# First modulations of a transformer block from stationary weight pages, with the first FFN products between them

## The chip, the cores and the metric

The kernel runs on one core of a Trainium2 chip. The metric is the device time of one execution in microseconds; where several executions are timed, the median is given. The core's engines each work through their own instructions in order: TensorE (PE for its products, PEld for the loads of its stationary operand), VectorE (DVE), ScalarE (ACT), GpSimd (POOL), and SyncE (SP), which here asks for the transfers. Sixteen DMA engines carry out what SP asks for.

## What is computed

The reference is one block of a diffusion backbone: 1024 latent tokens x and 256 context tokens ctx, both 1024 channels wide, in fp32. A modulation is a vector of 1024 numbers made from a conditioning vector; there are nine for the latents (from c) and nine for the context (from c_ctx). The first sublayer needs modulations 0 (shift) and 1 (scale):

```python
mods   = split(silu(c)     @ w_ada + b_ada, 9)      # latent tokens
mods_c = split(silu(c_ctx) @ w_ada + b_ada, 9)      # context tokens
h  = x + grid_pos_emb
h  = ffn_sublayer(h,   mods[0],   mods[1],   mods[2],   g_ffn1, w_ffn1_in, w_ffn1_out)
hc = ffn_sublayer(ctx, mods_c[0], mods_c[1], mods_c[2], g_ffn1, w_ffn1_in, w_ffn1_out)
...

def ffn_sublayer(h, shift, scale, gate, g, w_in, w_out):
    hn = rmsnorm(h, g) * (1 + scale) + shift
    a, b = split(hn @ w_in, 2)
    return h + 0.5 * gate * ((silu(a) * b) @ w_out)
```

Behind it come an mLSTM beside a gated chunk mixer, a second such FFN and a last norm. The change leaves all that as it is.

## The kernel before, in words

All activations lie with channels on the 128 partitions: h[tb][d] is the latents' channel block d of 8 in token half tb, hc[d] the context's (256 tokens). An fp32 product is made of three products of rounded parts: each operand is split into a high part (ACT casts) and a low part (VectorE subtracts, `split`, L145 and L146), and `mm3` (L182) issues high x high, high x low and low x high into one PSUM bank.

The head of the program makes modulations 0 and 1 and normalises the context. The 2 x 1024 columns of w_ada are cut into four quarters `qt` of 256 columns of each modulation and four parts `kp` of two row blocks; `ada_page` asks for 32 pieces of 256 KB with runs of 1 KB. Three quarters go over TensorE with silu(c) and silu(c_ctx) as two stationary columns and a page of 512 columns moving (`ada_rows`, L851); the two rows that come out are copied by ACT (`ada_copy`, L855) and turned into columns by four small products (`ada_flip`, L860). The fourth quarter is summed by VectorE (`side`, L792 and L794), transposed, reduced and spread by a product (L798, L799, L868). `ada_done` and `ada_side` add the bias and make the scale; `mod0` (L932 to L935) then applies scale and shift to two context blocks at a time and splits them into `hnc`. The junk products of `idle` (L923) keep TensorE at work meanwhile.

Then the loop over f (22 blocks of the FFN's width) multiplies the context by the first FFN's input weights: two tiles of 128 x 1024 a block (`wa` for a, `wb` for b), 24 products a tile, into the banks pa and pb, two blocks to a bank. `Weights` brings the tiles: `load` asks for one (`raw`, 512 KB), splits it into one of three `hl` buffers and keeps three ahead; every second pair of tiles has its raw page in the pool of the old modulation pages. The last two context blocks are only modulated while the first products run (`last0`). While the loop runs, the pages of x come in (L1020, one channel block in two halves for each f up to 8), the positions are added to them (`add_pos`, L917) and their squares summed for the latents' norm (L209, L210): these jobs stand in the list `todo` and `mm3` issues one after so many products, by a credit that each product adds to. The norm's row of the latents is then made by p (L215) and rb (L231).

The order on TensorE, VectorE and ACT in the head is the one in which the code is written: a `manual_schedule` from the start of the head to the end of f = 0. GpSimd and SP are not under it: the scheduler sets their order there, and that of all engines after it. The page of the positions (`pos`) is asked for (L1006) in the code just behind the head, ahead of the loop.

Of the kernel before, what the change touches and what calls it, by code (L numbers as in the profile page):

```python
# [55 lines left out]
def _build(ctx, tc, nc, a, out):  # L56
# [50 lines left out]
    class Weights:  # L107


        def __init__(self, order, name):  # L110
            self.c = ExitStack()
            self.pool = self.c.enter_context(tc.tile_pool(name=name, bufs=1, reuse_waits="tile"))
            self.order = deque(order)
            self.ready = deque()
            self.held = 0
            self.n = 0

        def load(self):
            n, i, w = self.order.popleft()
            src = a[n][i]  # L120
            if self.n % 4 < 2:
                raw = self.pool.tile([128, w], F32, name="raw", tag="raw", bufs=2)
            else:
                raw = hnp.tile([128, w], F32, name="raw", tag="pg0" if self.n == 2 else "pg1", bufs=8)
# [655 lines left out]
    def ada_load(page, m, hf, k):  # L780
        pgt = page()
        o = m * 1024 + hf * 512
# [53 lines left out]
    NQ = 4  # L836
    QW = 1024 // NQ
    QD = QW // 128
    KP = 512 // QW

    def ada_page(qt, kp, tag):
        pg = hnp.tile([128, KP, 2, QW], F32, name="adapg", tag=tag, bufs=8)
        for i in range(KP):
            src = a["w_ada"][kp * KP + i].rearrange("p (m c) -> p m c", m=9)[:, 0:2, qt * QW:(qt + 1) * QW]
            nc.sync.dma_start(pg[:, i], src)
        return [pg[:, i].rearrange("p m c -> p (m c)") for i in range(KP)]

    def ada_rows(pr, pgs, kp):
        for i, pg in enumerate(pgs):
            k = kp * KP + i  # L850
            T.matmul(pr[0:2, 0:2 * QW], sc2[:, :, k], pg, start=k == 0, stop=k == NKT - 1, skip_group_check=True)  # L851

    def ada_copy(pr):
        row = t2("adrow", shape=(2, 2 * QW))
        S.copy(row, pr[0:2, 0:2 * QW])  # L855
        return row

    def ada_flip(pc, row):
        for j in range(2 * QD):
            T.matmul(pc[:, 2 * j:2 * j + 2], row[:, j * 128:(j + 1) * 128], ident[0:2, 0:2], start=True, stop=True,  # L860
                     skip_group_check=True)

    def ada_side(qt, reds):
        bv = vs_("b_ada").rearrange("p (m d) -> p m d", m=9)
        cs = slice(qt * QD, (qt + 1) * QD)
        p8 = sm_ps("p8")
        for q, red in enumerate(reds):
            T.matmul(p8[:, q * 16:q * 16 + 16], grp4, red[:, 0:16], start=True, stop=True)  # L868
        for q in (1, 0):
            for r in range(4):  # L870
                sl = slice(32 * r, 32 * r + 32)
                V.tensor_add(mods[sl, 0:2, q, cs],
                             p8[sl, q * 16:q * 16 + 16].rearrange("p (m d r) -> p m d r", m=2, r=4)[:, :, :, r], bv[sl, 0:2, cs])
            scale_mod(0, 1, q, "g_ffn1", cs)

    def ada_done(qt, pc):
        sl = slice(qt * QD, (qt + 1) * QD)
        bv = vs_("b_ada").rearrange("p (m d) -> p m d", m=9)
        for q in (1, 0):
            V.tensor_add(mods[:, 0:2, q, sl],  # L880
                         pc[:, 0:4 * QD].rearrange("p (m d q) -> p m d q", m=2, q=2)[:, :, :, q], bv[:, 0:2, sl])
            done = scale_mod(0, 1, q, "g_ffn1", sl)
        return done
# [22 lines left out]
    def load_c(hcp, n):  # L906
        for i, pg in enumerate(hcp):
            nc.sync.dma_start(pg, a["cT"][i * n:(i + 1) * n].rearrange("d p t -> p d t"))
# [20 lines left out]
    def mod0(*ds):  # L929
        ts = [t2("nt")[:, 0:256] for _ in ds]  # L930
        for d, t in zip(ds, ts):
            S.activation(t, hc[d], AF.Identity, bias=mods[:, 0, 1, d:d + 1], scale=smod[:, 0, 1, d:d + 1])  # L932
            S.copy(hnc[d][:, 0, :], t)
        for d, t in zip(ds, ts):
            (V if d % 2 else G).tensor_tensor(hnc[d][:, 1, :], t, hnc[d][:, 0, :].bitcast(F32), ALU.subtract)  # L935

    def scaled0():
        for d in range(NKT):
            V.tensor_tensor(hc[d], hc[d], nct.rb, ALU.mult)
# [3 lines left out]
    sides = [t2("adacc") for _ in range(2)]  # L943

    def side(kp, pgs):
        for i, pg in enumerate(pgs):
            for q in range(2):
                ada_acc(V, sides[q], pg, q, kp * KP + i, kp + i == 0)

    load_c(hcp, 4)  # L950
    pgs = {}
    for qt, kp in ((2, 0), (0, 0), (0, 1), (2, 1), (0, 2), (0, 3), (2, 2), (1, 0), (1, 1), (2, 3), (1, 2), (1, 3),
                   (3, 0), (3, 1), (3, 2), (3, 3)):
        pgs[qt, kp] = ada_page(qt, kp, "pg1" if qt % 2 else "pg0")
    idle(30)
    for d in range(NKT):
        nct.sq(d)
    side(0, pgs[2, 0])
    prs = {0: mm_ps("adr")}
    ada_rows(prs[0], pgs[0, 0], 0)  # L960
    nct.rstd()
    ada_rows(prs[0], pgs[0, 1], 1)
    idle(3)
    side(1, pgs[2, 1])
    ada_rows(prs[0], pgs[0, 2], 2)
    nct.bcast()
    ada_rows(prs[0], pgs[0, 3], 3)
    row = ada_copy(prs[0])
    scaled0()
    side(2, pgs[2, 2])  # L970
    idle(4)
    pc = sm_ps("adc")
    ada_flip(pc, row)
    ada_done(0, pc)
    mod0(0, 1)
    prs[1] = mm_ps("adr")
    for kp in range(NKT // KP):
        ada_rows(prs[1], pgs[1, kp], kp)
    row = ada_copy(prs[1])
    side(3, pgs[2, 3])  # L980
    reds = [cp.tile([128, 32], F32, name="adred", tag="adred", bufs=2) for _ in range(2)]
    for acc, red in zip(sides, reds):
        ada_red(acc, red, 0)
    prs[3] = mm_ps("adr")
    ada_rows(prs[3], pgs[3, 0], 0)
    pc = sm_ps("adc")
    ada_flip(pc, row)
    ada_done(1, pc)
    mod0(2, 3)
    ada_rows(prs[3], pgs[3, 1], 1)  # L990
    ada_side(2, reds)
    for kp in (2, 3):
        ada_rows(prs[3], pgs[3, kp], kp)
    W.load()
    mod0(4, 5)
    row = ada_copy(prs[3])
    W.load()

    def last0():
        pc = sm_ps("adc")  # L1000
        ada_flip(pc, row)
        ada_done(3, pc)
        mod0(6, 7)
        W.load()
# [12 lines left out]
    for f in range(NF):  # L1017
        if 0 < f <= NKT:
            for tb in range(2):
                nc.sync.dma_start(h[tb][f - 1], a["xT"][f - 1, :, tb * 512:(tb + 1) * 512])  # L1020
        if 2 <= f < 2 + NKT:
            for tb in range(2):
# [13 lines left out]
        wa = W.take("w1i", 2 * f)  # L1036
        wb = W.take("w1i", 2 * f + 1)
        if f % 2 == 0:
            pa, pb = mm_ps("pa"), mm_ps("pb")
# [1367 lines left out]
```

## Time and profile before

| | us |
|---|---|
| median of 3 runs | 2641.32 |
| lowest and highest of them | 2641.31, 2643.13 |
| the profiled execution, its own time | 2639.9 |
| its span | 2638.1 |

The groups of the profile give: line, engine and operation, what is written from what (buffer numbers left out), the shape of one instruction, how many; then busy time in us and the mean of one in ns; then idle time of the engine ahead of them and what ended it. A timeline row gives the start, the time and the same names; a row of the chain the start, the time and the place. A row of the windows gives for a stretch of the span the busy time of each engine with its instructions, then the clock granted to TensorE (1.00 is full), the mean busy share of the DMA engines and the GB/s that they moved.

### The profile page before, as it was taken

The numbers are of one execution on the slowest core, as the hardware profiler recorded it, in microseconds if no ns is written. First come the engines' busy times: TensorE is split into PE (matmuls) and PEld (weight loads), VectorE is DVE, ScalarE is ACT, GpSimd is POOL, SyncE is SP. The second block draws the span as 40 slices with busy tenths as digits, with TensorE's granted clock in tenths as the row PEclk, the third lists the DMA queues.
The fourth block names the chain that finished last, engine by engine and source line by source line (L and its number), as shares of the span: only waits on it lengthen the run. The fifth ranks groups of instructions, "written<-read, shape, count | busy, mean of one in ns | idle before, by whom it ended". The sixth has DMA issues, their size and how long they took to land.

```text
span 2638.1 us, 35899 instructions
## 1 busy us (share of the span) xinstructions
PE 2621.8 (99%) x12856; PEld 2205.1 (84%) x12856; DVE 1978.8 (75%) x3546; ACT 1205.6 (46%) x2175; POOL 75.8 (3%) x158
## 2 busy tenths in 40 slices
PE   9999999999999999999999999999999999999998
PEld 6998888888889878888888888888887888888887
DVE  7988688687989646777765878778799766665855
ACT  5664344444347525564443454333346444344433
POOL 0000000000000000000000002221000000000000
PEclk9999999999999999999999999999999999999999
DMA  9833344368587222346653566546341333337644
GB/s 312 311 113 127 128 164 161 117 224 307 169 283 268 77 80 85 111 162 205 196 172 112 166 206 247 180 150 206 125 157 39 128 136 123 113 125 282 199 159 177
DMA packets 200083, 448.54 MB, mean 170 GB/s; under 512 B 20192, under 2 KB 54496, under 8 KB 199904
## 3 DMA queue, kind: packets, MB, share of 16 engines
q1 hardware_dynamic: 199472, 445.85, 49.6%
q8 instruction: 101, 1.65, 0.3%
q14 instruction: 78, 0.64, 0.1%
q10 hardware_dynamic: 432, 0.39, 0.0%
HBM read 324.92 MB, written 121.32 MB: 169 GB/s over the span
## 4 chain that ended last, share of the span: by engine, by line
PE 93%; DVE 2%; issue 2%; DMA 2%; ACT 1%; SPq 0%; POOL 0%; POOLq 0%; ACTq 0%; DVEq 0%
PE qa L412 18%; PE pq L1380 17%; PE po L536 13%; PE qb L412 13%; PE pt L1864 6%; PE pr L1299 6%; PE po L2239 3%; PE pa L182 2%; PE pc L1166 2%; PE pb L182 2%; PE pn L2024 2%; PE pu L1700 1%; PE pn L2022 1%; PE pkc L1359 1%; PE pvc L1456 1%
## 5 line engine op out<-in xcount | busy, mean ns | idle before, releaser
L146 DVE TENSOR_TENSOR ring<-rawq,ring 128x512 fp32r<-128x512 f32 x408 | 281.3, 690 | 221.2 <-ACT ring L145 218.5
L536 PE MATMUL po<-gring,wring 128*128 128x512 f32 (+1 forms) x1896 | 424.0, 384 | 0.1
L536 PEld LDWEIGHTS po<-gring,wring 128*128 128x128 f32 x1896 | 349.4, 188 | 70.8 <-ACT px L693 0.9
L145 ACT CAST ring<-rawq 128x512 fp32r<-128x512 f32 x408 | 253.4, 622 | 309.2 <-PE pq L1380 86.1
L412 PE MATMUL qa<-fc,ring 128*128 128x512 f32 x1056 | 252.3, 389 | 0.0
L412 PEld LDWEIGHTS qa<-fc,ring 128*128 128x128 f32 x1056 | 198.2, 188 | 41.4 <-DVE fc L146 0.4
L1380 PE MATMUL pq<-fc,ring 128*128 128x512 f32 x864 | 207.3, 392 | 0.0
L145 ACT CAST wring<-rw 128x512 fp32r<-128x512 f32 x154 | 95.7, 622 | 216.6 <-PE po L536 184.7
L1380 PEld LDWEIGHTS pq<-fc,ring 128*128 128x128 f32 x864 | 161.4, 188 | 33.0
L1864 PE MATMUL pt<-yp,ring 128*128 128x512 f32 x768 | 184.4, 394 | 0.0
L1864 PEld LDWEIGHTS pt<-yp,ring 128*128 128x128 f32 x768 | 143.0, 188 | 28.2
L146 DVE TENSOR_TENSOR wring<-rw,wring 128x512 fp32r<-128x512 f32 x154 | 105.6, 686 | 80.7 <-ACT wring L145 80.5
L1380 PE MATMUL pq<-fa,ring 128*128 128x512 f32 x576 | 141.9, 394 | 0.0
L1380 PE MATMUL pq<-fb,ring 128*128 128x512 f32 x576 | 136.8, 391 | 0.0
L412 PE MATMUL qa<-fa,ring 128*128 128x512 f32 x528 | 129.6, 395 | 3.5 <-DVE ring L146 3.5
L412 PE MATMUL qa<-fb,ring 128*128 128x512 f32 x528 | 126.8, 390 | 0.0
L412 PE MATMUL qb<-fb,ring 128*128 128x512 f32 x528 | 126.6, 389 | 0.0
L1380 PEld LDWEIGHTS pq<-fb,ring 128*128 128x128 f32 x576 | 107.5, 188 | 22.4 <-issue 0.2
L412 PE MATMUL qb<-fc,ring 128*128 128x512 f32 x528 | 126.2, 389 | 0.0
L412 PE MATMUL qb<-fa,ring 128*128 128x512 f32 x528 | 126.2, 389 | 0.0
L1380 PEld LDWEIGHTS pq<-fa,ring 128*128 128x128 f32 x576 | 106.9, 188 | 21.9 <-DVE ring L146 0.2
L794 DVE SCALAR_TENSOR_TENSOR adacc<-adapg,sc,adacc 128x512 f32<-128x512 f32 x154 | 111.8, 747 | 17.8 <-DMA adapg<-in_w_ada_dram 17.0
(380 smaller groups left out, 4671.5 us busy)
## 6 DMA issues: line engine op xcount, KB each, us to landing
adapg<-in_w_ada_dram SPq DMA_DIRECT2D x144, 256.0 KB, 3.7
fsp<-fhl SPq DMA_DIRECT2D x66, 512.0 KB, 2.7
gring<-fsp SPq DMA_DIRECT2D x66, 512.0 KB, 4.3
raw<-in_w1i_dram SPq DMA_DIRECT2D x44, 512.0 KB, 5.4
graw<-fsp SPq DMA_DIRECT2D x88, 256.0 KB, 3.2
rawq<-in_w1i_dram SPq DMA_DIRECT2D x38, 512.0 KB, 3.7
rawq<-in_w2i_dram SPq DMA_DIRECT2D x38, 512.0 KB, 3.4
fsp<-p SPq DMA_DIRECT2D x66, 256.0 KB, 2.1
```

The lines of the kernel that those rows point to most:

```text
L145: hi = S.copy(hl[:, 0, :], src)
L146: return hi, V.tensor_sub(hl[:, 1, :], src, hl[:, 0, :].bitcast(F32))
L182: T.matmul(pt, x, y, start=first and i == 0, stop=i == n - 1, skip_group_check=True)
L412: T.matmul(pt, hl[:, x, sl], pages[p][k][:, y, :], start=first and i == 0, stop=i == 11, skip_group_check=not first)
L536: T.matmul(pt[:, cs], w[:, x, sl], g[:, y, cs], start=grp and kp == 0 and i == 0, stop=kp == NFP - 1 and i == 2, skip_group_check=not grp)
L794: eng.scalar_tensor_tensor(acc, pgt, sc2[:, q, k:k + 1], acc, ALU.mult, ALU.add)
L1166: T.matmul(pt, hl[d // 4][:, x, sl], g[:, y, :], start=f == 0 and d % 2 == 0 and i == 0, stop=f == NF - 1 and i == 2, skip_group_check=True)
L1299: T.matmul(self.pt[m], pg[:, x, sl], hl[:, y, :], start=first and k == 0 and i == 0, stop=k == 3 and i == 2, skip_group_check=not first)
L1380: T.matmul(pt, hl[:, x, k * 128:(k + 1) * 128], pg[k][:, y, :], start=first and k == 0 and i == 0, stop=k == 3 and i == 2, skip_group_chec ...
L1864: T.matmul(pt, hl[:, x, k * 128:(k + 1) * 128], pg[:, y, :], start=kh + k + i == 0, stop=kh == 1 and k == 3 and i == 2)
L2024: T.matmul(pn[:, 0:257], qi[:, c_, :], self.C[d][:, c_, :], start=False, stop=c_ == 1)
L2239: T.matmul(pt, hl[:, x, k * 128:(k + 1) * 128], FO[p][k][:, y, :], start=first and k == 0 and i == 0, stop=k == 3 and i == 2, skip_group_c ...
```

## The change

Modulations 0 and 1 of the context come from pages of 128 output columns with all 1024 rows. Of the 16 such pages, eleven (`UNITS`, laid out in a tensor w_adaU of their own) are stationary operands: for each of the eight row blocks a product with silu(c) and silu(c_ctx) as two moving columns, so that both modulations come out as columns (`unit`). Five (`SIDE`, w_adaT, transposed) are multiplied with a row and summed by VectorE in one instruction (`side`): the row is silu(c_ctx) spread over the partitions by eight products (`spread`, scB[1]), and later silu(c) (scB[0]), which goes out to memory (scq) and comes back to all partitions. These five sums for silu(c) are jobs in `todo` from f = 2 on, ahead of the additions of positions.

The squares of the context are taken two blocks at a time. Each context block is modulated when its modulations are there, and the products of it with the first four weight tiles follow at once (`first`), between the pages. `Weights` gets a `fetch` that only asks for a tile, five `hl` buffers for three, and keeps five ahead. All transfers of the head, five tiles among them, are written ahead of it in one list. The loop over f begins at 1, and its products at 2. w_ada keeps modulations 2 to 8; ctx is laid out so that its pages are runs of 4 KB.

```diff
-        def load(self):
+        def fetch(self):
             n, i, w = self.order.popleft()
...
-            hl = self.pool.tile([128, 2, w], F32R, name="hl", tag="hl", bufs=3)
+            self.raws.append((n, i, w, raw))
+
+        def load(self):
+            if not self.raws:
+                self.fetch()
+            n, i, w, raw = self.raws.popleft()
+            hl = self.pool.tile([128, 2, w], F32R, name="hl", tag="hl", bufs=5)
             split(hl, raw)
...
-            while self.order and self.held < 3:
+            while (self.raws or self.order) and self.held < 5:
                 self.load()
...
+    for u in ("hc0", (1, 0), "hc1", (1, 1), (0, 0), (1, 2), (0, 1), (1, 3), (0, 2), "W", (0, 3), (1, 4), "W", (0, 4), (1, 5),
+              (0, 5), "W", (1, 6), (0, 6), "W", (1, 7), (0, 7), "W"):
+        if u == "W":
+            W.fetch()
...
+        if u == (1, 2):
+            nc.sync.dma_start(scq, sc2[:, 0, :])
+    nc.sync.dma_start(scB[0], scq.rearrange("p k -> (p k)").partition_broadcast(128))
...
+    def side(m, d, q):
+        V.tensor_tensor_reduce(waste, page[m, d], scB[q], 1.0, vs_("b_ada")[:, m * 8 + d:m * 8 + d + 1], ALU.mult, ALU.add,
+                               mods[:, m, q, d:d + 1])
...
+        for k in range(NKT):
+            T.matmul(col[m, d], page[m, d][:, k * 128:(k + 1) * 128], sc2[:, :, k], start=k == 0, stop=k == NKT - 1,
+                     skip_group_check=True)
...
+    first(0, 1, 3)
+    first(0, 0, 4)
+    first(0, 1, 4)
+    first(1, 0, 0, 1)
+    first(0, 0, 5)
+    unit(1, 7)
+    side(0, 7, 1)
+    unit_done(1, 7)
+    mod0(7)
+    W.load()
...
+    first(0, 0, 7)
+    first(0, 1, 7)
+    W.done(2)
+    first(1, 0, 4, 5, 6, 7)
+    W.done()
+    first(1, 1, 4, 5, 6, 7)
+    W.done()
+    order.close()
 
     nc.sync.dma_start(pos, a["pos"])
...
-    for f in range(NF):
-        if 0 < f <= NKT:
+    for f in range(1, NF):
+        if f <= NKT:
...
         if 2 <= f < 2 + NKT:
+            if f - 2 < len(SIDE):
+                slow(side, *SIDE[f - 2], 0)
             for tb in range(2):
                 slow(add_pos, tb, f - 2)
```

Two places of the order that comes out of this matter below. The first is SP's, from the last modulation page on. Before, the two last pieces of w_ada (adapg) are followed by weight tiles (raw) in the order of use, by the rest of the constants (cst), the positions (pos) and the halves of x (h):

```order
L845 DMA adapg_187<-in_w_ada_dram 128x2x256 x2
L126 DMA raw_386<-in_w1i_dram 128x1024
L126 DMA raw_401<-in_w1i_dram 128x1024
L1007 DMA cst_86<-in_cst_dram 128x384
L126 DMA raw_445<-in_w1i_dram 128x1024
L1006 DMA pos_130<-in_pos_dram 128x320
L126 DMA raw_474<-in_w1i_dram 128x1024
L126 DMA raw_485<-in_w1i_dram 128x1024
L1020 DMA h_112<-in_xT_dram 128x512
L1020 DMA h_120<-in_xT_dram 128x512
```

After, behind the last page (adaT_182) come the broadcast row, the constants, halves of x and then tiles; raw_184 is the first tile of f = 2 (its split is hl_455), while raw_496, raw_513 and raw_611 are its third, its fourth and one of f = 5:

```order
L914 DMA adaT_182<-in_w_adaT_dram 128x1024
L926 DMA scB_136<-scq_139 128x1024
L1063 DMA cst_86<-in_cst_dram 128x384
L1076 DMA h_112<-in_xT_dram 128x512
L1076 DMA h_120<-in_xT_dram 128x512
L1076 DMA h_113<-in_xT_dram 128x512
L1076 DMA h_121<-in_xT_dram 128x512
L127 DMA raw_496<-in_w1i_dram 128x1024
L127 DMA raw_513<-in_w1i_dram 128x1024
L127 DMA raw_611<-in_w1i_dram 128x1024
L1076 DMA h_114<-in_xT_dram 128x512
L127 DMA raw_184<-in_w1i_dram 128x1024
```

Then follow nine more halves of x and five more tiles, the rows below the last of them; here are the positions, and what stands behind (raw_530 and raw_579 are the tiles of f = 4):

```order
L1076 DMA h_125<-in_xT_dram 128x512
L127 DMA raw_902<-in_w1i_dram 128x1024
L1076 DMA h_118<-in_xT_dram 128x512
L1076 DMA h_126<-in_xT_dram 128x512
L1062 DMA pos_130<-in_pos_dram 128x320
L127 DMA raw_935<-in_w1i_dram 128x1024
L1076 DMA h_119<-in_xT_dram 128x512
L1076 DMA h_127<-in_xT_dram 128x512
L378 DMA rawh_1401<-in_w1i_dram 128x1024
L127 DMA raw_530<-in_w1i_dram 128x1024
L127 DMA raw_579<-in_w1i_dram 128x1024
```

The positions moved from the place ahead of all halves of x to one behind 14 of the 16, and the tiles no longer stand in the order of use. 50 transfers now stand ahead of the positions.

The second place is VectorE's, at the end of the head. The semaphores that an instruction waits for stand in brackets; each DMAHW counts every eighth of SP's transfers. Before, the first addition of positions stands behind the last split of the context (hnc_135) and ahead of the splits of the third to fifth tile:

```order
L935 TENSOR_TENSOR hnc_135<-nt_438,hnc_135 128x256 [waits Activation_49]
L917 TENSOR_TENSOR h_112<-h_112,pos_130 128x512 [waits DMAHW3_49,DMAHW0_49]
L146 TENSOR_TENSOR hl_447<-raw_445,hl_447 128x1024 [waits DMAHW7_49,Activation_49]
L146 TENSOR_TENSOR hl_476<-raw_474,hl_476 128x1024 [waits DMAHW1_49,Activation_49]
L146 TENSOR_TENSOR hl_487<-raw_485,hl_487 128x1024 [waits DMAHW2_49,Activation_49]
```

After, it stands behind the last sum of a page for silu(c_ctx), the first for silu(c) and the last split of the context, and ahead of the splits of f = 2 and f = 3:

```order
L937 ISA waste_138,mods_101<-adaT_182,scB_137,vec_84 128x1024 [waits DMAHW0_49,DVE_49]
L937 ISA mods_101 128x1
L955 TENSOR_SCALAR smod_103<-adc_440,bias1_140,vec_84 128x2 [waits PE_49]
L937 ISA waste_138,mods_101<-adaT_147,scB_136,vec_84 128x1024 [waits DMAHW1_49,DVE_49]
L937 ISA mods_101 128x1
L895 TENSOR_TENSOR hnc_135<-nt_451,hnc_135 128x256 [waits Activation_49]
L879 TENSOR_TENSOR h_112<-h_112,pos_130 128x512 [waits DMAHW3_49,DMAHW2_49]
L153 TENSOR_TENSOR hl_455<-raw_184,hl_455 128x1024 [waits DMAHW3_49,Activation_49]
L153 TENSOR_TENSOR hl_493<-raw_491,hl_493 128x1024 [waits DMAHW1_49,Activation_49]
L153 TENSOR_TENSOR hl_498<-raw_496,hl_498 128x1024 [waits DMAHW7_49,Activation_49]
L153 TENSOR_TENSOR hl_515<-raw_513,hl_515 128x1024 [waits DMAHW0_49,Activation_49]
```

The addition kept its place between the context's last split and the next tiles, but its second DMAHW wait is now the count that the transfer of the positions completes (the seventh on DMAHW2).

From the end of the first loop on, the rows of all engines are the same before and after but for the numbers of lines and buffers, and the second request for ctx, whose runs are longer.

More of the change, by code (lines that the diff above doesn't have):

```diff
@@ L966, in _build @@
+    unit(0, 1)
+    unit(1, 3)
     nct.bcast()
[L967 to L993, printed above, removed]
[L994 to L1004 removed]
+    for u in ((1, 0), (1, 1), (0, 1)):
+        unit_done(*u)
```

233 lines of the change are left out of this document (140 added, 93 removed).

## The prediction
> **What bounds the kernel now.** I read the page first, then the chain of work that ended last, then the stage before the chain becomes plain.
>
> ```profile
> span 2638.1 us, 35899 instructions
> PE 2621.8 (99%) x12856; PEld 2205.1 (84%) x12856; DVE 1978.8 (75%) x3546; ACT 1205.6 (46%) x2175; POOL 75.8 (3%) x158
> ...
> 37.38 2.18 PE pa L182 x16
> 39.55 0.98 PE adc L860 x8
> 40.53 2.35 PE pb L182 x18
> ...
> 50.95 2.88 PE pa L182 x24
> 53.83 2.88 PE pb L182 x24
> 56.71 2.88 PE pa L182 x24
> ```
>
> TensorE is busy 99% of the span, and in the chain each weight tile of the context's first FFN (24 products, 2.88 us) follows the last without a gap. I number these tiles n0, n1, ... in the order of use: n0 and n1 are f = 0, and n4 is the first of f = 2. In the chain n4 starts at 50.95; its third product, the first that needs the low half of its weights, comes 2 x 0.12 = 0.24 us later, at 51.2. All that stands on TensorE after n4 is the same before and after the change, as far as the order of instructions tells. So I measure the change by one number: **how much later or earlier does n4's third product run**, plus what TensorE loses behind it.
>
> **The front, which the change rewrites, has cover.** What it adds on TensorE is cheap: the eleven stationary pages are 8 products of 2 columns each, and an fp32 product is two passes, each about one weight load.
>
> ```profile
> 97.47 0.98 PEld L215 LDWEIGHTS p<-ones,acc 128*128 128x128 f32 x8
> L146 DVE TENSOR_TENSOR hl<-raw,hl 128x1024 fp32r<-128x1024 f32 x6 | 7.2, 1224 | 0.7 <-ACT hl L145 0.6
> L794 DVE SCALAR_TENSOR_TENSOR adacc<-adapg,sc,adacc 128x512 f32<-128x512 f32 x14 | 9.6, 746 | 0.0
> L932 ACT ACTIVATE nt<-hc,mods,smod 128x256 f32<-128x256 f32 x8 | 4.8, 598 | 10.0 <-DVE mods L880 6.5 <-DVE smod L888 3.6
> ```
>
> 0.98 / 8 = 0.12 us a load, so 11 x 16 x 0.12 = 21 us, with 96 products of n0 to n3 another 11.5. It takes away 24 row products, the flips, two transposes and two reductions, none of which is on the path once the pages decide. The sum of a page on VectorE has no row; the nearest are the two-input pass over 128x1024 (1.22 us) and two fused passes over 512 (2 x 0.75 = 1.49), and its small second instruction is like the other tiny ones, 0.16. I take 1.4, between 1.2 and 1.7.
>
> The front ends with the last of the pages. Up to it SP asks for 22 transfers of 512 KB and 0.24 MB of small ones, 11.8 MB. At the pace found below (400 GB/s from 2.8 us, 2 us to land) it lands at 34.2. Behind it stand its sum (1.4), the scale (0.16), ACT's two passes (0.6 + 0.4), one more page sum on VectorE (1.4) and the low half (0.54): 38.7. Then 30 products of n0 to n3 are left, 3.6 us: **42 us**, nine before n4's start now. That is what the change could win. Were the front's cover gone, a microsecond in it would cost a microsecond; but I find it covered by 16 us of another wait.
>
> **The term that decides: the positions.** VectorE works in order. In the changed order the first addition of positions to h stands ahead of the low half of n4, and it waits for the transfer of the positions. Now SP asks for that transfer ahead of every page of x; in the changed order, where SP's queue is left to the scheduler, 25 transfers stand between the last modulation page and it: the broadcast row, the rest of the constants, 14 half pages of x, 9 weight tiles.
>
> ```profile
> 30.47 0.33 SPq L1006 DMA_DIRECT2D pos<-in_pos_dram  x1
> 37.73 0.90 SPq L1020 DMA_DIRECT2D h<-in_xT_dram  x2
> 43.38 0.69 DVE L917 TENSOR_TENSOR h<-h,pos 128x512 f32<-128x512 f32 x1
> pos<-in_pos_dram SPq DMA_DIRECT2D x1, 160.0 KB, 7.0
> ```
>
> Here the request goes out at 30.47 and lands 7.0 later, long before the addition at 43.38. After: up to and with the positions SP asks for 32 x 524,288 + 14 x 262,144 bytes and 0.60 MB of small ones, **21.05 MB**. When is that through? The windows give the pace.
>
> ```profile
> 0.00:5.00 5.00, 4.01 (x19) 4.01 (x20) 0.23 (x1) 3.48 (x7) 0.44 (x6) 1.00 0.52 156
> 10.00:15.00 5.00, 5.00 (x19) 1.77 (x18) 4.09 (x16) 0.40 (x2) 0.00 (x0) 1.00 1.09 348
> 31.50:33.00 1.50, 1.50 (x7) 0.48 (x5) 0.72 (x5) 0.91 (x2) 0.00 (x0) 1.00 1.00 394
> 33.00:34.50 1.50, 1.50 (x6) 0.44 (x7) 0.43 (x2) 1.47 (x4) 0.72 (x1) 1.00 1.04 399
> 34.50:36.00 1.50, 1.50 (x5) 0.28 (x4) 1.33 (x9) 1.19 (x3) 0.00 (x0) 1.00 1.07 408
> 36.00:38.00 2.00, 1.80 (x9) 0.93 (x8) 1.99 (x3) 1.97 (x5) 1.49 (x1) 1.00 0.31 120
> 40.00:45.00 5.00, 4.97 (x37) 4.44 (x36) 2.52 (x7) 3.81 (x6) 0.74 (x1) 1.00 1.00 366
> 41.00:42.00 1.00, 1.00 (x10) 1.00 (x9) 0.16 (x1) 0.95 (x3) 0.00 (x0) 1.00 1.11 438
> ```
>
> The last number is GB/s, the one before the share of the DMA engines. With w_ada in runs of 1 KB the full engines move 348. With weight tiles, whose runs are 4 KB as those of the new pages are, they move 394 to 408; with half pages of x (2 KB) among them 366. 156 x 5 = 0.78 MB by 5 us is 2.2 us of full pace, so it begins at 2.8. I take 400 for the 16.8 MB of large ones (42.0 us), 366 for x (10.0) and 348 for the small (1.7): 53.7, begun at 2.8. A transfer lands after its bytes: the positions land at 30.47 + 7.0 = 37.5, while the engines have gone quiet by 36. With 2 us for that: 2.8 + 53.7 + 2.0 = **58.5**. Then the addition (0.69), the split of n4 (1.23) and 0.1 for the hand-over: the third product at 60.5, against 51.2. **+9.3 us.** Ends: were the whole at 348 with the same landing, 60.5 + 4.8 = 65.3 for the positions, so +16.1; at the best single row (438, no landing time) 50.9, so +1.7.
>
> The Trainium skill, "DMA: Bandwidth & Descriptors", section Specifications, gives an HBM limit of about 358 GB/s per core. By it the positions would land at 2.8 + 58.8 + 2.0 = 63.6 (an estimate from that page) and this term be +14.4. The rows from 31.5 to 36 stand above it, so I go by the rows.
>
> **The clock behind the wait.** TensorE will stand idle from 42 to 60. Before has one such wait, later:
>
> ```profile
> PE qa L412 <- DVE ring L146: 3.5, 1, 3.5
> 1980.00:1985.00 5.00, 5.00 (x24) 3.99 (x22) 5.00 (x9) 4.12 (x8) 0.00 (x0) 1.00 0.47 161
> 1985.00:1990.00 5.00, 1.50 (x5) 1.08 (x4) 4.82 (x9) 2.72 (x5) 0.00 (x0) 0.86 0.43 157
> 1990.00:1995.00 5.00, 5.00 (x17) 3.97 (x17) 3.86 (x10) 0.20 (x1) 0.00 (x0) 0.50 0.00 0
> 1995.00:2000.00 5.00, 5.00 (x22) 4.07 (x21) 3.29 (x9) 3.37 (x8) 0.00 (x0) 0.96 0.00 2
> ```
>
> The clock (third number from the end) was 0.86, 0.50 and 0.96 in the windows after 3.5 idle us: at half clock for 1.4 + 5.0 + 0.4 = 6.8 us. At 0.50, 17 products ran where 24 ran before: 7/24 of 6.8 is **+2.0**, which I take. Ends: 3.4 if the 256-column products of this stage lose half, and 1 if a good part of the slow time lies in the wait itself.
>
> **VectorE behind the wait.** It restarts with a debt.
>
> ```profile
> 47.42 1.89 DVE L917 TENSOR_TENSOR h<-h,pos 128x512 f32<-128x512 f32 x3
> 49.43 1.23 DVE L146 TENSOR_TENSOR hl<-raw,hl 128x1024 fp32r<-128x1024 f32 x1
> ...
> sum 110.00, PE 110.00 PEld 109.54 DVE 100.84 ACT 76.40 POOL 0.00; mean PE 22.00 PEld 21.91 DVE 20.17 ACT 15.28 POOL 0.00
> ...
> 105.51 0.19 PEld L231 LDWEIGHTS rb<-diag,onesr 128*128 128x128 f32 x1 [0.19 <-ACT diag L225]
> ```
>
> When n4 starts now, VectorE has done four additions of positions and the split of n5; after, one addition and the split of n4: 3 x 0.65 + 1.23 = 3.2 us owed. Four page sums with silu(c) come too, 4 x 1.4 = 5.6, the fifth lying in the wait. That is 8.8 us, and the sum over 50 to 160 leaves VectorE 110 - 100.84 = 9.2 us of idle. But TensorE's product of the norm's row waits for VectorE's chain without slack (0.19 at 105.51), and in the changed order it stands only two tiles (5.8 us) later. 8.8 - 5.8 = **+3.0**; ends: 0, if the idle and the five split buffers carry it, and 8.8, if nothing does.
>
> **Sum.** 9.3 + 2.0 + 3.0 = +14.3. The profiled execution took 2639.9 us (span 2638.1 and 1.8 around it), 1.4 below the median 2641.32 of the runs shown. 2639.9 + 14.3 = 2654.2, with the median's 1.4 it would be 2655.6; I say **2655**.
>
> **Rivals.**
> - **The old pace holds** (the engines move 348 with x, the broadcast of one row and the constants mixed in). For: 366 in the window with x. Against: 394 to 408. Then +16.1 + 2 + 3: 2661. The HBM rule of the Trainium skill named above points here.
> - **VectorE becomes the bound** after the restart, with the whole debt paid by TensorE: +9.3 + 2 + 8.8: 2660. For: no slack at 105.51. Against: 9.2 us of idle, and buffers for two more splits.
> - **The wait for the positions does not bite** (their transfer lands early), but the tiles are late. n4's tile, with 15.9 MB up to it, then lands at 2.8 + 39.8 + 2 = 44.5 and its third product runs at 46.8, in time; but n8 is the 56th of SP's transfers, with 23.1 MB up to it: 2.8 + 57.8 + 2 = 62.6, with cast (1.05) and split 64.9, where now, four tiles after n4, its third product runs at 62.7. +2.2: 2642, no change; at 438 it would be -3.8, 2636, no change either. For: the diff says nothing of the positions. Against: VectorE's order names that transfer.
> - **It does what it says, faster:** n0 to n3 done at 42 and the tiles behind them there in the order of use, so n4 at 42 in place of 51: -9, 2631. It decides if the chip's SP asks for tiles as they are needed and not as the changed order has them. For: it does so now. Against: now the order has them so too.
>
> **How the numbers follow.** Forecast 0.62, old pace 0.18, VectorE 0.10, no bite 0.07, as it says 0.03. Low end: 408 throughout and 1 us to land (+6.3), clock 1, VectorE 0: 2647, and 1 lower for the page sum's unknown. High end: the old pace's 2661 with the clock at 3.4 and some of VectorE's debt: 2665. That holds the forecast and most of the first two rivals, 0.8 together. 0.2% is 5.3 us, about what a measurement of this kernel can tell from no change. Slower 0.90, same 0.07, faster 0.03.
>
> **What would show it.** In the chain of the changed kernel: an addition of positions to h ahead of n4's split, released by a DMA at 57 to 60; TensorE waiting 14 to 20 us for it, once; granted clock 0.5 in the 5 us behind; n0 to n3 done by 40 to 45; windows of 380 to 410 GB/s until the positions land; a second, smaller wait of TensorE near the norm's row, around 125. A wait of less than 5 us, or n4 running before 52, would make the prediction wrong.

## The result and the profile after

| | before | changed |
|---|---|---|
| median, us (runs) | 2641.32 (5) | 2685.43 (5) |
| lowest and highest | 2639.43, 2643.43 | 2680.61, 2686.94 |
| ratio, 95% interval | | 1.0161 [1.0146, 1.0176] |
| profiled execution: span, us | 2638.1 | 2684.3 |

The changed kernel is 44 us slower; 14 were forecast. The spans differ by 46.2 us. I read first the head of the program, where the forecast put everything. The chain of work of the changed kernel around n4 (start, us, what):

```profile
14.31 10.24 PE adc L950 x48
24.55 0.64 PE rb L238 x2
25.18 6.63 PE adc L950 x32
...
50.29 6.13 DMA raw<-in_w1i_dram
56.43 1.23 DVE hl L153
57.70 2.88 PE pa L189 x22
60.58 2.84 PE pb L189 x24
...
176.29 8.21 PE qa L419 x36
```

The pages' own products (adc) stand in the chain for 10.24 and 6.63 us. n4's third product runs at 57.70, where it ran at 51.0: **+6.7 us**. The first product of the latents' FFN (qa) starts at 176.29; the same row of the kernel before:

```profile
169.23 8.19 PE qa L412 x36
```

That is +7.1 us at the end of the context's loop. **The other 39.1 us come behind it, where both kernels have the same instructions in the same order.** The two timelines of VectorE and TensorE show what n4 waited for:

```profile
51.66 0.42 DVE L895 TENSOR_TENSOR hnc<-nt,hnc 128x256 fp32r<-128x256 f32 x1
55.82 0.69 DVE L879 TENSOR_TENSOR h<-h,pos 128x512 f32<-128x512 f32 x1 [3.74 <-DMA pos<-in_pos_dram]
56.43 4.62 DVE L153 TENSOR_TENSOR hl<-raw,hl 128x1024 fp32r<-128x1024 f32 x4
```

```profile
55.14 1.58 PE L189 MATMUL pb<-hnc,hl 128*128 128x256 f32 x12
56.56 0.39 PE L189 MATMUL pa<-hnc,hl 128*128 128x256 f32 x2
57.70 2.88 PE L189 MATMUL pa<-hnc,hl 128*128 128x256 f32 x22 [0.75 <-DVE hl L153]
```

VectorE stalls at the addition of positions, as forecast (3.74 us, until 55.8). But TensorE comes to n4 only at 56.56 and waits 0.75 us. Why it comes so late stands in the windows (third number from the end: granted clock; last: GB/s):

```profile
5.00:10.00 5.00, 5.00 (x42) 5.00 (x42) 0.00 (x0) 1.83 (x4) 0.00 (x0) 1.00 1.02 411
10.00:15.00 5.00, 4.20 (x31) 4.12 (x31) 4.16 (x10) 1.33 (x3) 0.00 (x0) 0.79 1.04 419
15.00:20.00 5.00, 5.00 (x25) 5.00 (x25) 1.88 (x10) 1.74 (x3) 0.00 (x0) 0.50 1.03 416
40.00:45.00 5.00, 5.00 (x31) 5.00 (x30) 3.93 (x8) 1.97 (x3) 0.00 (x0) 0.64 1.04 412
45.00:50.00 5.00, 5.00 (x45) 5.00 (x45) 2.71 (x5) 1.01 (x2) 1.76 (x1) 1.00 1.03 410
300.00:400.00 100.00, 100.00 (x434) 81.01 (x433) 77.83 (x123) 41.22 (x71) 0.00 (x0) 1.00 0.44 150
700.00:800.00 100.00, 100.00 (x449) 82.91 (x448) 87.48 (x155) 36.91 (x65) 0.00 (x0) 1.00 0.74 240
```

From 13 to 43 us TensorE ran at half its clock, though it was busy 5.00 of 5.00 us; before, the clock stood at 1.00 there. The transfers moved 410 to 419 GB/s in these rows, more than the 400 of the forecast.

The last two rows belong to the 39 us. Here are the same stretches of the kernel before:

```profile
300.00:400.00 100.00, 100.00 (x443) 82.84 (x442) 76.61 (x121) 40.99 (x71) 0.00 (x0) 1.00 0.41 142
700.00:800.00 100.00, 100.00 (x449) 82.97 (x448) 87.86 (x155) 43.93 (x78) 0.00 (x0) 1.00 0.79 263
```

In 100 us of the latents' first loop TensorE did 443 products before and does 434 now, never idle, at clock 1.00 in both. In the output stage (700 to 800) it does 449 in both. So a product got slower, in some stages only. By the starts of products in the traces, a product of 512 columns follows the last after 226.9 ns on average before and after 230.6 now, over some 9,080 such pairs: 3.69 x 9,080 = **33.5 us**. The remaining 5.6 are taken up at the end.

What can slow a product whose operands have the same shapes? Their place. The change adds `bias1`, 8 floats a partition, among the constants. Pools grow from both ends of the on-chip memory; all that grows from the low end behind it lies 32 bytes further, and what grows from the high end stays. Start bytes in a partition, from the two programs (in brackets modulo 256):

```
                        before           changed
ring, a low slot        101,344 (224)    101,376 (0)
fa or fb, a slot         11,232 (224)     11,264 (0)
fc, first slot          180,192 (224)    180,192 (224)
```

Before, moving and stationary operand start alike modulo 256 in all but some 30 of these pairs. Now about half the pairs start 32 or 224 apart, and in the trace just these follow after 233.4 ns, the others after 228.0. That is a correlation; the experiments had to show it.

### The profile page after: what moved, and what is told of

Its sections match the earlier page's. It is cut to its first block, busy times and chain, and to the rows that moved or that the text cites. A ratio compares the mean times of both kernels' runs of the same rounds, so it can differ in the third digit from the quotient of the medians.

```text
span 2684.3 us, 35996 instructions
## 1 busy us (share of the span) xinstructions
PE 2662.7 (99%) x12930; PEld 2228.7 (83%) x12930; DVE 1982.7 (74%) x3529; ACT 1204.6 (45%) x2170; POOL 76.7 (3%) x158
## 4 chain that ended last, share of the span: by engine, by line
PE 91%; DVE 4%; DMA 2%; issue 2%; ACT 1%; POOL 0%; SPq 0%; POOLq 0%; ACTq 0%; DVEq 0%
PE qa L419 18%; PE pq L1434 17%; PE po L543 14%; PE qb L419 14%; PE pr L1353 6%; PE pt L1918 6%; PE po L2293 3%; PE pn L2078 2%; PE pb L189 2%; PE pa L189 2%; PE pu L1754 1%; PE pn L2076 1%; PE pkc L1413 1%; PE pvc L1510 1%; DVE wring L153 1%
## 5 line engine op out<-in xcount | busy, mean ns | idle before, releaser
L153 DVE TENSOR_TENSOR ring<-rawq,ring 128x512 fp32r<-128x512 f32 x408 | 281.6, 691 | 230.2 <-ACT ring L152 228.2
L419 PEld LDWEIGHTS qa<-fa,ring 128*128 128x128 f32 x528 | 101.4, 193 | 27.6 <-DVE ring L153 3.9
```

The lines of the kernel that those rows point to most:

```text
L153: return hi, V.tensor_sub(hl[:, 1, :], src, hl[:, 0, :].bitcast(F32))
L419: T.matmul(pt, hl[:, x, sl], pages[p][k][:, y, :], start=first and i == 0, stop=i == 11, skip_group_check=not first)
```

## Experiments on the 39 us: where the tiles lie

One line decides the place in most of these runs, a pad that stands among the constants in both kernels:

```diff
-    cp.tile([128, 32], F32, name="pad")
+    cp.tile([128, 40], F32, name="pad")
```

**The changed kernel 64 bytes off** (with this line; 32 + 32):

> The changed kernel with a pad of 160 instead of 128 bytes among the constants, so that everything behind it lies 64 bytes, and not 32, further than in the kernel before. Nothing else differs. In the changed kernel's trace the loss comes in two parts: 6 to 7 us up to the end of the context's loop (n4 starts at 57.7 for 51.0), and 39 us more behind it, where the instructions are the same before and after: there a product of 512 columns follows the last after 233 ns where the moving and the stationary tile start at different places modulo 64 bytes, and after 227 ns where they start alike (before: all alike, 226.8). Theory 1, the 32 bytes of the new small tile for bias1 do that: with 64 the 33 us or so of slower products go, the head stays, so 2646 to 2653 us. Theory 2, the layout of the weights in memory, the clock or the transfers do it: 2680 to 2687 as the changed kernel.

2676.89 us, 8.5 less and not 35: neither theory. Modulo 64 all operands start alike in this run, so "modulo 64" fell; spacing still 230.2 ns.

**The kernel before, 32 bytes off** (the same line):

> The kernel before, its pad of 128 bytes made 160: everything behind it lies 32 bytes further, as in the changed kernel. Theory 1 (different starts modulo 64 bytes of the two operands cost 6 to 7 ns a product): 2641 + 30 to 37 = 2671 to 2678 us, with spacings of 231 to 236 ns from 200 to 585 us and 227 in the output stage of the FFN. Theory 2 (something else that the change brings): 2639 to 2644.

2672.74 us, +31.1. Nothing but the place of tiles was touched, and the loss is there. Its windows:

```profile
300.00:400.00 100.00, 100.00 (x433) 81.01 (x432) 76.42 (x121) 40.03 (x69) 0.00 (x0) 1.00 0.42 142
700.00:800.00 100.00, 100.00 (x448) 82.95 (x447) 87.25 (x154) 41.46 (x73) 0.00 (x0) 1.00 0.78 264
```

433 products where before had 443, and none lost in the output stage, as in the changed kernel: there `gring` and `wring` moved together.

**The kernel before, 64 bytes off** (48 floats):

> The kernel before with its pad made 192 bytes: 64 bytes further. Theory 1: all starts stay alike modulo 64, 2639 to 2644 us. Rival: any move of the tiles disturbs something (banks of a larger period), then 2650 or more.

2664.12 us, +22.5: the rival was right, the period is longer than 64.

**Both ends 32 bytes off** in the changed kernel, one more line ahead of the pools at the high end:

```diff
+    pool("rpad", side="right").tile([128, 8], F32, name="rpad")
     fx = pool("fx", side="right")
```

> The changed kernel, with a tile of 32 bytes ahead of the pools that grow from the other end too, so that all operands of the large products start at 0 modulo 64 (in the kernel before all start at 32, in the changed one some at 0 and some at 32). Theory 1 in this form, the difference of the two starts decides: 2646 to 2653 us like the run with 64 bytes. Rival: a start at 0 is the slow one by itself: 2685 or above, up to 2700 since more operands start there.

2676.22 us. The high end grows downwards, so the two ends moved 64 bytes apart, not together: I had thought of modulo 64 alone. The time is that of the other run with a distance of 64 (2676.89).

**No shift** (the pad of the changed kernel at 24 floats, which makes room for bias1):

> The changed kernel with its pad made 96 instead of 128 bytes: the 32 bytes of bias1 are taken out of the pad, so that every tile behind lies where it lay before the change. The runs with shifts of 32 and 64 bytes showed products of 512 columns 227 ns apart where the two operands start alike modulo 256 bytes, 233 where they differ by 32, 64, 192 or 224. Theory 1 (the shift is the loss behind the head): 9,080 products x 3.7 ns = 33.6 us go, 2685.4 - 33.6 = 2652, the same as 2641.5 + 6.5 (start of n4) + 1.5 (debt of VectorE) = 2649.5; so 2647 to 2654. Theory 2 (a part of the loss is in the change itself, such as the clock): 2660 or more.

2653.02 us, as the first theory said: 32.4 of the 44 us are gone. From 300 to 400 us TensorE does 442 products again, where the changed kernel had 434 and the kernel before 443:

```profile
300.00:400.00 100.00, 100.00 (x442) 82.80 (x442) 80.21 (x128) 42.38 (x73) 0.00 (x0) 1.00 0.45 156
```

**128 bytes** (64 floats, the kernel before, one time):

> The kernel before, everything behind its pad 128 bytes further. If the period of the disturbance is 128 bytes: products of 512 columns at 226.8 ns, 2639 to 2644 us. If it is 256 or more: 230 ns and above in the first FFN's loop, 2650 to 2680 us.

2667.46 us. The two runs that follow tell "distance modulo 256" from "any departure from the old places": **256 bytes** in the kernel before (96 floats), and the changed kernel with its 32 bytes left in and an `rpad` of 56 floats, by which every large operand starts at 0 modulo 256.

> The kernel before, everything behind its pad 256 bytes further (shifts of 32, 64 and 128 took 31, 22 and 26 us). If the period is 256 bytes, as the products with distances of 256 modulo 512 in the trace of before say (227.3 ns), the time is that of before: 2639 to 2644. If any shift between the two ends of the memory costs: 2660 or more.

> The changed kernel with its shift of 32 bytes left in, and a tile of 224 bytes ahead of the pools that grow from the other end, so that all operands of the large products start at 0 modulo 256 (at 224 in the kernel before). If only the distance of the two operands modulo 256 decides: 512-column products at 227 ns and the time of the changed kernel without a shift, 2649 to 2656. If the place itself matters (224 is good, others not): 2670 or more.

2640.76 and 2653.82 us: both as without a shift. For products of 512 columns the common place (224 or 0) made no difference, the distance of the two operands modulo 256 did. Together, with the mean spacing of the 9,080 pairs of products of 512 columns (about half of the pairs have the distance named, the rest 0):

| kernel and distance | spacing, ns | median, us |
|---|---|---|
| before, 0 | 226.9 | 2641.3 |
| before, 256 (0 modulo 256) | 226.9 | 2640.8 |
| before, 64 | 230.2 | 2664.1 |
| before, 128 | 230.1 | 2667.5 |
| before, 32 | 230.6 | 2672.7 |
| changed, 0 | 226.9 | 2653.0 |
| changed, all at 0 modulo 256 | 226.9 | 2653.8 |
| changed, 64 | 230.2 | 2676.9 |
| changed as given, 32 | 230.6 | 2685.4 |

The times are not in the order of the spacings, because products of 256 columns go the other way: they follow each other more closely at a distance (120.0 ns at 0, 118.3 at 224 in the changed kernel). In the kernel before, 64 bytes off, the 9,080 pairs lose 29.5 us and some 1,500 products of 256 columns win 7.8 (114.6 for 119.8 ns on average); the time rose by 22.5.

The groups of products of the latents' first loop (200 to 560 us) show the same in the mean of one: the changed kernel, and the run with all at 0.

```profile
L419 PE MATMUL qa<-fc,ring 128*128 128x512 f32 x468 | 114.2, 394 | 0.0
```

```profile
L419 PE MATMUL qa<-fc,ring 128*128 128x512 f32 x474 | 113.1, 389 | 0.0
```

A profile shows this in two signs only: fewer products in a stretch that is 100% busy, and a mean of one that grew by about 1%. Nothing waits, so no view of waits names it.

The Trainium skill, "SBUF — State Buffer", section "SBUF: two separate sides", says of TensorE and ScalarE and of VectorE's own port pair that they "never wait on anyone". That is said of engines that contend with one another, and it leaves open what the two operands of one product do. Here their distance decides the spacing, while the other engines do the same work in the runs with and without a shift. Why it does, no run shows.

## Experiments on the head: positions, clock, tiles

All but the last of these are the changed kernel without a shift, so 2653.02 us is what they are measured against.

**More columns.** To keep the array busy, the pages' moving operand is 64 columns in place of 2.

```diff
-            T.matmul(col[m, d], ..., sc2[:, :, k], ...)
+            T.matmul(wide, ..., sc2[:, :, k].unsqueeze(1).to_broadcast([128, 32, 2]), ...)
```

> As the run without a shift, but the moving operand of the stationary pages is 64 columns (the two columns repeated 32 times) in place of 2. Theory A, the clock is halved because products of 2 columns leave the array nearly idle: granted clock 1.00 in the windows of 10 to 45 us, n0 to n3 done at 42 to 47 in place of 56.9; then TensorE waits for the positions and n4's third product runs at about 57.7 as before, so the time is within 2 us of the run without a shift, or up to 3 more if the clock falls in that wait. Rival: the clock follows something else (the load of weights): it stays at 0.50, the pages take longer if anything, 0 to 5 us more.

2652.72 us. The clock fell all the same, as the rival said, though the time did not rise. One of its windows, and its wait at n4:

```profile
15.00:20.00 5.00, 5.00 (x25) 5.00 (x25) 2.12 (x9) 1.74 (x3) 0.00 (x0) 0.50 1.02 406
```

```profile
54.39 0.40 PE L189 MATMUL pa<-hnc,hl 128*128 128x256 f32 x2
59.02 1.23 PE L189 MATMUL pa<-hnc,hl 128*128 128x256 f32 x4 [4.24 <-DVE hl L153]
```

TensorE came 2.5 us earlier than without the edit (54.39 for 56.85) and waited 4.24 us, until the positions were added. So the front and the positions end close together: n4 waits 0.75 us in the changed kernel, 1.94 in it without a shift, 4.24 here.

**Early positions.** Their request, with that of the rest of the constants, is moved into the head's list, behind the second page of the context. The lines below show the positions alone.

```diff
+            if u == "hc1":
+                nc.sync.dma_start(pos, a["pos"])
...
-    nc.sync.dma_start(pos, a["pos"])
```

> As the run without a shift, and the positions and the rest of the constants are asked for early, right behind the second page of the context. In the changed kernel VectorE waited 3.7 us for the positions (to 55.8), but TensorE, at half its clock from 13 to 43 us, came to n4 only at 56.95 and then waited 0.75 us. Theory A, the half clock bounds the front: only the 0.75 us and a part of VectorE's 3.7 us of debt go, 1 to 4 us less than without a shift. Theory B, the recorded prediction, the positions bound it: 9 us or more less.

2674.59 us, 21.6 *more*, which neither theory had. VectorE's timeline:

```profile
12.63 0.69 DVE L982 TENSOR_TENSOR sq<-sq 128x512 f32<-128x512 f32 x1
35.75 0.69 DVE L879 TENSOR_TENSOR h<-h,pos 128x512 f32<-128x512 f32 x1 [22.43 <-DMA h<-in_xT_dram]
36.36 0.42 DVE L984 TENSOR_TENSOR acc<-sq 128x256 f32<-128x256 f32 x1
```

With the positions early the scheduler put the first addition into the middle of the head, ahead of the context's norm, and there it waits 22.4 us for a page of x, with the whole head behind it. The run says nothing of its theories, but it prices the mechanism of the forecast: one misplaced wait in VectorE's order, 22 us.

**Early positions, the additions held** behind the head's last split:

```diff
+    def add_late(tb, d):
+        with tc.issue_after(low[7].ins):
+            add_pos(tb, d)
```

> As the run without a shift, the positions asked for behind the second page of the context, and this time the additions of positions are held behind the last split of the context on VectorE, as in the changed kernel (in the run before this one they had slipped into the head and waited there for pages of x to 35.7 us). Theory A, TensorE at half clock bounds the front: it comes to n4 at about 56.9 as in the changed kernel and starts it without a wait; with VectorE's 3.7 us of debt gone too, 2649 to 2652 us for 2653. Theory B, the recorded prediction, the positions bound it: n4 at 48 or earlier, 2644 us or less.

2649.82 us. n4 starts at 56.33 and no longer waits, and yet the loop ends at 177.5 us as without the edit (177.4):

```profile
56.33 3.04 PE L189 MATMUL pa<-hnc,hl 128*128 128x256 f32 x24
```

```profile
PE p L222 <- DVE acc L217: 1.4, 1, 1.4
PE rb L238 <- ACT diag L232: 0.8, 1, 0.8
PE rb L238 <- DVE diag L233: 0.2, 1, 0.2
```

n4's third product runs 2.6 us earlier (56.57 for 59.19). TensorE gives 2.4 us back at the products of the norm's row (the waits above, between 100 and 125 us), where it had no wait without the edit. So the positions were not what held the head: theory A for n4's start. That the half clock held it, the next runs show.

**Early positions and a busy array:** behind each page four products of 512 columns that nothing reads.

```diff
+        for _ in range(4):
+            T.matmul(junk, onesr, onesr.unsqueeze(1).to_broadcast([128, 4, 128]), start=True, stop=True)
```

> As the run before, and behind each of the eleven stationary pages four products of 512 columns whose result nothing reads, with 64 columns in place of 2 in the pages' own products: some 70% of a page's time the array then streams columns. If the clock follows the streaming (64 columns alone, 46%, did not hold it): 1.00 throughout, n0 to n3 done at 44 to 48; then the tile n8, SP's 56th transfer, is late (23.1 MB at 412 GB/s from 2.8 us, 2 us to land, cast and split: third product at about 63, as before the change), so 2642 to 2647 us. If the clock falls nevertheless, the 44 added products cost 10 us or more of the front at half clock: 2655 to 2665.

2655.29 us, where 2642 to 2647 was expected: the clock held through the head, and the gain was given back. Window and timeline:

```profile
15.00:20.00 5.00, 5.00 (x39) 4.64 (x38) 2.68 (x14) 0.96 (x3) 0.00 (x0) 1.00 1.03 407
```

```profile
52.15 3.04 PE L189 MATMUL pa<-hnc,hl 128*128 128x256 f32 x24
55.03 3.04 PE L189 MATMUL pb<-hnc,hl 128*128 128x256 f32 x24
57.91 3.04 PE L189 MATMUL pa<-hnc,hl 128*128 128x256 f32 x24
60.79 3.04 PE L189 MATMUL pb<-hnc,hl 128*128 128x256 f32 x24
66.27 0.50 PE L189 MATMUL pa<-hnc,hl 128*128 128x256 f32 x2 [2.44 <-ACT hl L152]
67.53 2.72 PE L189 MATMUL pa<-hnc,hl 128*128 128x256 f32 x11 [0.76 <-DVE hl L153]
```

n4 at 52.15, four tiles, and then n8 is late: its third product at 67.5, where the expectation had 63. With it come half clock for 3.4 us from 67.0 and, later, a wait of 3.62 us for VectorE at the norm's product (114.91) and half clock for 10.2 us from there; the next run has none of these. The shares of streaming in this expectation and in the last one of this group (46, 70 and 59%) are estimates that no view shows. Clock 1.00 at 15 to 20 us needed the long products behind each page, not just rows full of busy time. The Trainium skill, "TensorE: Matmul & The Clock Gate", section "Part 1: The HAM clock gate", has the clock follow how busy TensorE was in free windows of 3.4 us. The lengths agree (30.7 us at half clock in the changed kernel is nine of them); that weight loads with 2 or 64 columns behind each do not hold the clock, though TensorE's rows are full, is what these runs add.

**The tiles in order** on top of it: each tile is asked for behind the one used before it, and halves of x behind the tile of the next block.

```diff
+                with tc.issue_after(W.asked[2 * f + 2].ins):
                     nc.sync.dma_start(h[tb][f - 1], ...)
```

> As the run before, and the tiles are asked for in the order of use, and halves of x only behind the tile that is used in the block after their own. If the clock holds: no late tile, n4 at 44 to 49 and n8 in time, 6 to 10 us less than the run before less VectorE's debt: 2633 to 2641 us, below the kernel before. If the order of the transfers was not the next bound: the same time as the run before.

2644.70 us, ratio to the kernel before 1.0011 [1.0002, 1.0020]. n8 is in time, and 10.6 us go: the order of the transfers was the next bound, some 3.6 us at n8 itself, and the rest with the wait and the half clock behind it. n4 started at 52.7, so the expected range was missed by the front, not by a wait.

**Two unread products in place of four:**

> As the run with early positions, a busy array and the tiles in order (2644.7, n4 started at 52.7 for 50.8 in the kernel before), with two unread products of 512 columns behind each page in place of four. They lie on the path there: 22 products x 0.23 = 5 us less if the clock holds at 59% streaming: n4 at 48 to 50, 2639 to 2642 us. If the clock falls: n4 at 54 or later, 2646 to 2650. If the front is bound by its transfers (the last page lands at about 35) and VectorE and not by these products: n4 at 51 to 52.7, 2642 to 2645.

2642.36 us, ratio 1.0001 [0.9991, 1.0011]. n4 starts at 49.6 and the loop ends at 168.0, 1.1 us ahead of the kernel before. So the products did lie on the path, and the clock held but for one window of 3.4 us. The median fell by 2.3 us, where 5 were expected. With the shift, the late positions, the half clock and the order of the tiles mended in this way, which itself puts 22 unread products on the path, the change is worth nothing that can be measured.

**A version that beats both.** The runs on the place of tiles had shown a second thing: products of 256 columns are *slower* at distance 0 (120.0 ns, and 113.4 to 118.6 at others). This run is measured against the kernel before (2641.40 us beside it). In that kernel, 64 bytes of pad at the start of the pool of the context's tiles move these alone:

```diff
+            self.pool.tile([128, 16], F32, name="wpad")
             self.order = deque(order)
```

> The kernel before with 64 bytes of pad at the start of the pool of the context loop's tiles alone, so that the weights of its 256-column products start 192 bytes modulo 256 from the activations, and all else lies where it lay. In the traces with such a distance these products stood 113.6 to 117.7 ns apart, 120.0 where both start alike: 1,056 products x 2.3 to 6.4 ns, so 2 to 7 us less: 2634.5 to 2639.5. If 256-column products are not affected by it: 2641.6.

2638.35 us, ratio 0.9986 [0.9978, 0.9995], faster than both kernels. A tile of the context's loop, in the timeline of this run and of the kernel before:

```profile
61.52 2.88 PE L183 MATMUL pa<-hnc,hl 128*128 128x256 f32 x24
64.24 2.88 PE L183 MATMUL pb<-hnc,hl 128*128 128x256 f32 x24
```

```profile
62.31 3.04 PE L182 MATMUL pa<-hnc,hl 128*128 128x256 f32 x24
65.19 3.04 PE L182 MATMUL pb<-hnc,hl 128*128 128x256 f32 x24
```

2.72 us from tile to tile in place of 2.88, up to the products of the norm's row (near 100 us); behind them it is 2.83, in the same run with the same pad. The loop ends at 165.2 for 169.1.

## Why the prediction was wrong, point by point

The sign was right, the size was not, and the step that failed is the first: "All that stands on TensorE after n4 is the same before and after the change, as far as the order of instructions tells. So I measure the change by one number". The same instructions in the same order took 39 us longer. The order says what runs, not where the operands lie, and the change's eight floats of `bias1` moved one of the two operands by 32 bytes in about half of the pairs. The runs show this term twice: -32.4 us when the shift is taken out of the changed kernel, +31.1 when it is put into the kernel before. The diff shows the new tile; I priced its instruction and not its bytes. The prediction's own sign of being wrong came true too, and with or without the shift: "A wait of less than 5 us" for the positions (0.75 us, and 1.94 without the shift).

Without the shift the changed kernel takes 2653.0, two below the forecast. That is in part luck. Of 13.1 us between the spans, 8.3 stand at the end of the context's loop, where 14.3 were forecast; 2.6 come near 1747 us, at a wait and 3.4 us of half clock, and the rest is open. The terms one by one:

- **Positions, forecast +9.3; measured +6.7 at n4's third product.** The stall is real and where it was said to be, and the positions landed at 55.8 for 58.5, since the transfers moved 408 to 420 GB/s up to 50 us. But it is not what set n4: held out of the way (2649.8), n4 still started at 56.3.
- **The front done at 42, forecast; it was done at 56.6.** The step took page products at 0.12 us a load and looked at the clock only behind the wait. They took 0.21 (10.24 us for 48 in the chain) and ran at half clock from 13 to 43 us. Even with the clock held the front ends at 49.6 (with 22 unread products on its path), so 42 was too early by other waits too, which no run separates.
- **Clock behind the wait, forecast +2.0; measured 0.** The clock was 1.00 from 45 us on, because the wait lasted 0.75 us and not 16. Where it lasted longer (4.24 us in the run with 64 columns) one window of 3.4 us at half clock followed.
- **VectorE's debt, forecast +3.0; measured +0.4** from n4's third product to the latents' first. In it are 1.6 us won by products of 256 columns (118.3 for 120.0 ns, 40 tiles), so some 2 of waits. In three runs with these products at 120 ns (the additions held, all at 0 modulo 256, no shift) n4's third product ran at 56.6, 57.4 and 59.2, and the loop ended at 177.3 to 177.5 all the same: TensorE waited 2.4, 1.3 and 0 us at the products of the norm's row. So VectorE's chain to the latents' norm set the end in the first two, and came just in time in the third. The rival "VectorE becomes the bound" had that wait; it priced the debt at 8.8 us.
- **"No bite, but the tiles are late"** came true when the positions and the clock had been mended: n8 stalled TensorE to 67.5 us. (Its -3.8 at 438 GB/s comes to -2.9 by its own terms, 2.8 + 52.7 + 2 + 2.3 for 62.7; no chance hangs on it.)
- **"As it says, faster"** rested on 42 us and on tiles in the order of use. The order had to be forced, the front came to 49.6 at best, and the gain was 1.1 us at the loop's end and none in the median.

Sum for the changed kernel: 6.7 + 0.4 + 33.5 = 40.6 of 46.2 us between the two spans. In the rest are two stretches of 3.4 us at half clock, near 1620 and 1764 us, where the distance to the kernel before grows by 2.4 and 2.3. Each stands at a wait of TensorE for VectorE, of 1.90 and 2.47 us; in the kernel before these two waits are 1.1 and 1.5 us long, and the clock stays at 1.00. The changed kernel 64 bytes off, with the same instructions, has neither stretch (its waits are 1.5 us and less). Why the waits are longer stays open.

## What to carry to other kernels

Before a change is priced by its instructions, see which tiles it moves: a new tile of a few bytes among the constants shifts every pool behind it, and where pools grow from two ends, pairs of operands change their distance in all later stages. Where products of 512 columns rule, allot small tiles in multiples of 256 bytes, or out of a pad, and take a time that changed where nothing changed (fewer products in a stretch that is 100% busy) as a question of place. And where stationary operands are loaded for a few moving columns, read the granted clock of that very stretch.

## What the runs showed of the hardware that I had not expected

- **The distance of the two operands.** Products of 512 columns follow each other after 226.9 ns where moving and stationary tile start alike modulo 256 bytes; at 32 or 224 after 233.4, at 64 after 231.2, at 128 after 232.8, at 192 after 233.3. Products of 256 columns go the other way: 120.0 ns at 0, 118.3 at 224, 118.6 at 128, and at 192 between 113.4 and 117.7, from run to run and from one part of a run to the next. Why the last varies was not tried.
- **A busy TensorE at half clock.** Weight loads with 2 or 64 columns behind each kept it at 5.00 of 5.00 us and at clock 0.50; two more products of 512 columns a page (0.45 us in some 2.2) held the clock but for one window.
- **Transfers mostly of 4 KB runs** moved 408 to 420 GB/s from 5 to 50 us; those of 1 KB runs 348 before. The Trainium skill, "DMA: Bandwidth & Descriptors", section Specifications, gives about 358 as the HBM limit per core, half of what a stack gives to two cores; one core alone went past it here.
